# HGRN2's chunk scan on TensorE: four groups of matmuls for each of the first seven heads, in place of sixteen small steps

## The chip, the cores and the metric

The kernel runs on one core of a Trainium2 chip. The metric is device time in microseconds of one execution, the median of the runs shown. A core has TensorE (PE, matmuls, with weight loads shown as PEld), VectorE (DVE), ScalarE (ACT), GpSimd (POOL) and SyncE (SP), which issues most of the DMAs. Each engine works through its own list of instructions in the order in which the program gives them, and waits on semaphores for the others.

## The reference

One step of a two-layer decoder: 512 prompt tokens and 64 sample tokens (8 sequences of 8), width 1024. Layer 0 mixes tokens by HGRN2, layer 1 by S5; each layer has a SwiGLU and an embedding part behind it. The change touches only HGRN2, which has 8 heads of 128 and computes, chunk by chunk:

```python
def step(s, xs):
    qc, kc, vc, lc = xs
    b = jnp.cumsum(lc, axis=1)
    bm = b[:, CHUNK // 2 - 1][:, None]
    bl = b[:, -1]
    qh = qc * jnp.exp(b - bm)
    kh = kc * jnp.exp(bm - b)
    att = jnp.where(causal, jnp.einsum('bthk,bshk->bhts', qh, kh), 0.0)
    o = (jnp.einsum('bhts,bshv->bthv', att, vc)
         + jnp.einsum('bthk,bhkv->bthv', qc * jnp.exp(b), s))
    s_new = (jnp.exp(bl)[..., None] * s
             + jnp.einsum('bshk,bshv->bhkv', kc * jnp.exp(bl[:, None] - b), vc))
    return s_new, o
...
q, fz, v, g = jnp.split(x @ w_in, 4, axis=-1)
f = lbf + (1.0 - lbf) * jax.nn.sigmoid(fz)
qh = heads(jax.nn.silu(q) * HG_QK_SCALE)
kh = heads(1.0 - f)
o, s = hgrn2_chunk_scan(qh, kh, heads(v), heads(jnp.log(f)), s0)
o = rms_norm(o, gnorm_w) * jax.nn.silu(heads(g))
return o @ w_out, s
```

The prompt starts from a zero state, the eight samples from stored ones; the new states are outputs (`hgp`, `hgs`).

## The kernel before, in words

The whole program is written in the order in which it is issued (`manual_schedule`); the functions below are Python generators, and where each yields decides what stands next to what on every engine.

All large products are done in three matmuls each (`mm3`, lines 299 to 301): a weight is split into a high and a low part (`whi`, by ScalarE on line 200, and `wlo`, by VectorE on line 203), and so is the input. Weights arrive by DMA from SP (`wraw`, line 226), 512 KB at a time, two buffers deep, and are split some steps ahead; `passed` counts the matmul triples and issues these splits.

`proj(h)` makes the projections of head h: for even h first V for two heads (40 triples of 256 columns), then in every head decay, query and gate, each 8 triples of 320 columns and 8 of 256. So an even head has 88 steps (n = 0 to 87) and an odd one 48. Behind each of the three a side generator is queued, `decay`, `factors` or `queries`, which does the elementwise work on ScalarE, VectorE and GpSimd, one piece per step. `decay` makes the exponentials `e`, `L` and `k` and four running sums `b`. `factors` makes KH, QH, KL, QL, K2 and E2. `queries` starts with nine empty steps (`QWAIT`), so it runs early in the next head's projections; it copies the gates, applies SiLU (with a table load ahead and one behind), and gives QH, QL and Q2 their final values.

The scan of head h is interleaved with the projections of head h + 1: the loop at the end of `hgrn` advances `scan(h)` after the steps listed in `SCAN_AT` (line 66), the first row beside even projections, the second beside odd ones. So scans of even heads run beside odd projections, which have fewer steps. A scan has these steps, with the lines by which the profile names them:

- transposes of K2, four tiles (L661) and the samples' tile (L668), each copied to `kT` by ScalarE
- kT x V (L674), and the chunk states `S` on VectorE; `hgp` is written
- the samples' state updates (L688), one into a `tr` bank and one into an `mm` bank, and `So` on VectorE in two halves; `hgs` is written
- scores in four steps: KH x QH for a tile of 128 tokens (L704) and seven small products KL x QL of 16, 32 and 64 columns (L709); then VectorE copies the unmasked part to `att` (L713)
- samples: Q2 x S0 (L719), copied to `oc`; their score (L725), copied to `ats` (L727)
- output: L732, L735 and, two steps later, L741 and L743; ScalarE squares it
- the mean square (L752), then `r` by Ln and Exp on ScalarE, and the scaling on VectorE

The kernel uses eight banks of PSUM: four `mm` for projections, two `tr`, one `o` and one `os` for the scan. A tile is a whole bank and the banks of a tag go round in turn. The program waits by tile: a matmul into a bank waits for the engine that last read that tile, whatever columns it read.

The last head's scan runs beside the output projection (`mix_out`, line 809).

Of the kernel before, what the change touches and what calls it, by code (L numbers as in the profile page):

```python
# [8 lines left out]
FP32 = mybir.dt.float32  # L9
# [3 lines left out]
ACT = mybir.ActivationFunctionType  # L13
OP = mybir.AluOpType
# [3 lines left out]
T = 576  # L18
NB = 288
NP = 512  # L20

HC = ((0, 320), (320, 576))
H = 8
# [39 lines left out]
SY = ((6, 8), (8, 8), (6, 10), (6, 2))  # L63
QY = ((3, 3), (2, 5), (1, 3), (1, 2))
SPLIT_S5 = 14
SCAN_AT = ((2, 4, 10, 16, 20, 26, 30, 34, 38, 42, 46, 50, 54, 60, 68, 74), (2, 4, 6, 9, 12, 15, 17, 19, 21, 23, 26, 33, 34, 36, 41, 45))
QWAIT = 9
SIDE = 1
OCT = 2
# [73 lines left out]
def hybrid_decoder_kernel(ctx: ExitStack, tc: tile.TileContext, a: dict):  # L143
    nc = tc.nc
# [6 lines left out]
    def bank(tag, bufs):  # L151
        return psum.tile([128, 512], FP32, tag=tag, name=tag, bufs=bufs)

    def mm_bank():
        return bank("mm", 4)

    def tr_bank():
        return bank("tr", 2)
# [3 lines left out]
    ident = cst[:, 0:128]  # L162
    vmask = cst[:, 128:132]
    idpat = cst[:, 136:152]
    gnw = cst[:, 152:153]
# [6 lines left out]
    EPS_LN, EPS_RMS, ONE, ZERO = (eps[:, i:i + 1] for i in range(4))  # L172
    ones = {}
# [13 lines left out]
    xfh = xf_t.rearrange("p (k c) -> p k c", k=KD)  # L187
# [8 lines left out]
    def act(out, in_, func, bias=None, scale=1.0):  # L196
        nc.scalar.activation(out, in_, func, bias=ZERO if bias is None else bias, scale=scale)  # L197

    def copy(out, in_):
        nc.scalar.activation(out, in_, ACT.Copy)  # L200

    def tt(out, x, y, op, eng=None):
        (eng or nc.vector).tensor_tensor(out, x, y, op=op)  # L203

    def stt(out, x, s, y, op0, op1):
        nc.vector.scalar_tensor_tensor(out, x, s, y, op0=op0, op1=op1)
# [148 lines left out]
    def run(g):  # L355
        for _ in g:
            pass

    def step(g, n=1):
        for _ in range(n):  # L360
            if next(g, StopIteration) is StopIteration:
                return False
        return True
# [109 lines left out]
    def hgrn():  # L473
        es = ExitStack()
        hp = es.enter_context(tc.tile_pool(name="hp", bufs=1))
        msk = hp.tile([128, 224], FP32, name="msk")
        nc.sync.dma_start(msk, a["cst"][:, 160:384])
        own = msk[:, 192:224]
        attm = msk[:, None, 0:128].bitcast(U32).to_broadcast([128, 4, 128])
        smask = msk[:, 128:192].bitcast(U32)  # L480
# [8 lines left out]
        att_sb, ats_sb = [], []  # L489
# [18 lines left out]
        def t576(tag, bufs=1):  # L508
            return hp.tile([128, T], FP32, tag=tag, name=tag, bufs=bufs)

        V = {}
        hd = {}
        sides = []
# [12 lines left out]
        def proj(h):  # L526
            if h % 2 == 0:
                p = take(16)
                V[h // 2] = hp.tile([128, 5, 256], FP32, tag="V", name="V", bufs=2)
                for i in range(5):  # L530
                    c = slice(i * 128, i * 128 + 128) if i < 4 else slice(T - 128, T)
                    ps = mm_bank()
                    for k in range(KD):
                        hi, lo = w_ap(p + 2 * k, 256)
                        mm3(ps[:, :256], xhih[:, k, c], xloh[:, k, c], hi, lo, k == 0, k == KD - 1)
                        yield
                    copy(V[h // 2][:, i, :], ps[:, :256])
                free_to(p + 16)
            d = hd[h] = {}

            yield from two_units(take(8))
            sides.append(decay(h, d, hd["ps"]))

            yield from two_units(take(8))
            sides.append(factors(d, hd["ps"]))
            yield from two_units(take(8))
            sides.append(queries(h, d, hd["ps"]))
# [12 lines left out]
        LEVELS = list(enumerate((16, 32, 64)))  # L560
# [92 lines left out]
        def scan(h):  # L653
# [106 lines left out]
            tt(o[:, NP:], ops[:, 0:64], r[:, NP:], OP.mult)  # L760
            yield

        nc.scalar.preload_act_table_set(LNEXP)
        g = None
        for h in range(H):
            at = SCAN_AT[h % 2]
            for n, _ in enumerate(proj(h)):
                if n % SIDE == 0 and sides and not step(sides[0]):
                    sides.pop(0)
                for _ in range(at.count(n) if g else 0):  # L770
                    step(g)
            if g:
                run(g)
            g = scan(h)

        xq.close()
        XS.append(ctx.enter_context(tc.tile_pool(name="xs", bufs=1, side="right")))
# [30 lines left out]

    def mix_out():
        es, g = hgrn()  # L810
        p0 = take(64)
        held = []
# [941 lines left out]
    with more_weights(3, (pos["i"] + 64) // 8):  # L1754
        start = ple_gate(1, pj, pp, SEGS, y_emit, GW[1])
# [140 lines left out]
```

## Time and profile before

| | |
|---|---|
| median of three runs | 1588.85 us (1588.47 to 1592.74) |
| profiled execution | 1589.6 us, its span 1587.8 us |
| TensorE busy | 1514.9 us, 95% |
| VectorE, ScalarE, GpSimd busy | 60%, 43%, 22% |
| mean granted clock of TensorE | 0.983 |
| scans of the first seven heads | from 50 to 312 us of the span |

A row of the timeline gives start, length, engine, line, operation, output<-inputs, shape and count; in square brackets stands the idle time of the engine ahead of it and what ended it. TensorE's fp32 matmuls are shown as two records each (L704, L741 and the like), the transposes as one. Matmuls overlap in the pipeline, so the distance from one start to the next tells their price, not their length. A row of the waits gives who waited for whom, the sum in us, how often, and the longest.

### The profile page before, as it was taken

Reading aid. Unit: us, or ns where it says so; the run is one execution under the profiler, and the core shown is the slowest. Engines: PE = TensorE matmul, PEld = TensorE weight load, DVE = VectorE, ACT = ScalarE, POOL = GpSimd, SP = SyncE. Lnnn points to the kernel's source line nnn. Section 1 sums busy time; section 2 is a strip of 40 time slices with the busy share of each in tenths; the row PEclk is TensorE's granted clock in tenths of the full one; section 3 lists DMA queues with packets and bytes.
Section 4 is the critical chain, followed back from the end, with each engine's and each line's share of the span. In section 5 each row is a group of like instructions: output and inputs, shape, how many; then the busy total and the mean of one; then the engine's idle time right before and its main releaser. Section 6 shows DMA issues by size and latency. Waiting matters only on the chain. (4 is left out here: it accounts for less than half of the span.)

```text
span 1587.8 us, 30040 instructions
## 1 busy us (share of the span) xinstructions
PE 1514.9 (95%) x12550; PEld 1467.1 (92%) x12550; DVE 947.1 (60%) x1711; ACT 687.9 (43%) x1152; POOL 342.9 (22%) x447
## 2 busy tenths in 40 slices
PE   8899999899999999999999947999999999999998
PEld 7898989788999999999989947899999999999997
DVE  4848484868547778953486699457433233334685
ACT  5546464746532223123278524436432222123375
POOL 1303030302003768860022332302000000000111
PEclk9999999999999999999999978999999999999999
DMA  5223131232224877663214986432222222223121
GB/s 185 95 69 101 63 109 64 100 115 80 68 70 145 216 185 216 195 182 108 98 54 170 233 209 179 101 107 80 67 80 93 80 81 93 81 80 120 31 78 60
DMA packets 97255, 180.32 MB, mean 114 GB/s; under 512 B 41888, under 2 KB 56912, under 8 KB 96864
## 3 DMA queue, kind: packets, MB, share of 16 engines
q1 hardware_dynamic: 88144, 151.92, 31.3%
q0 software_dynamic: 8976, 26.49, 6.2%
q8 instruction: 98, 1.61, 0.4%
q14 instruction: 37, 0.30, 0.1%
HBM read 151.08 MB, written 27.30 MB: 112 GB/s over the span
## 5 line engine op out<-in xcount | busy, mean ns | idle before, releaser
L299 PE MATMUL mm<-xh,whi 128*128 128x288 f32 x2048 | 609.7, 298 | 9.5 <-ACT xh L200 6.5
L300 PE MATMUL mm<-xl,whi 128*128 128x288 f32 x2048 | 608.9, 297 | 5.0 <-POOL xl L203 3.5
L301 PE MATMUL mm<-xh,wlo 128*128 128x288 f32 x2048 | 606.6, 296 | 1.3 <-DVE wlo L203 1.3
L299 PEld LDWEIGHTS mm<-xh,whi 128*128 128x128 f32 x2048 | 387.8, 189 | 15.9 <-ACT xh L200 7.6
L300 PEld LDWEIGHTS mm<-xl,whi 128*128 128x128 f32 x2048 | 387.9, 189 | 8.4 <-POOL xl L203 5.0
L301 PEld LDWEIGHTS mm<-xh,wlo 128*128 128x128 f32 x2048 | 387.8, 189 | 1.5 <-DVE wlo L203 1.5
L200 ACT ACTIVATE whi<-wraw 128x1024 fp32r<-128x1024 f32 x208 | 218.7, 1053 | 250.1 <-DMA wraw<-in_w_dram 117.2
L203 DVE TENSOR_TENSOR wlo<-wraw,whi 128x1024 fp32r<-128x1024 f32 x200 | 247.1, 1252 | 33.2 <-ACT whi L200 32.8
L299 PE MATMUL mm<-hhi,whi 128*128 128x288 f32 x704 | 209.3, 297 | 0.0
L301 PE MATMUL mm<-hhi,wlo 128*128 128x288 f32 x704 | 207.5, 295 | 0.0
L300 PE MATMUL mm<-hlo,whi 128*128 128x288 f32 x704 | 207.2, 294 | 0.0
L203 DVE TENSOR_TENSOR fs<-fs,mm 128x288 f32<-128x288 f32 x88 | 39.9, 454 | 254.5 <-PE mm L301 241.4
L203 POOL TENSOR_TENSOR ln_s<-ln_s,xf 128x288 f32<-128x288 f32 x24 | 24.3, 1012 | 570.9 <-DVE xf L203 451.2
L299 PEld LDWEIGHTS mm<-hhi,whi 128*128 128x128 f32 x704 | 132.1, 188 | 1.7 <-issue 1.4
L300 PEld LDWEIGHTS mm<-hlo,whi 128*128 128x128 f32 x704 | 132.1, 188 | 0.3
L301 PEld LDWEIGHTS mm<-hhi,wlo 128*128 128x128 f32 x704 | 132.0, 188 | 0.0
L299 PE MATMUL mm<-xhi,whi 128*128 128x320 f32 (+1 forms) x384 | 121.5, 316 | 0.0
L300 PE MATMUL mm<-xlo,whi 128*128 128x320 f32 (+1 forms) x384 | 113.3, 295 | 0.0
L301 PE MATMUL mm<-xhi,wlo 128*128 128x320 f32 (+1 forms) x384 | 113.2, 295 | 0.0
L200 ACT ACTIVATE hhi<-fs 128x288 fp32r<-128x288 f32 x88 | 38.8, 441 | 152.1 <-DVE fs L203 152.1
L197 ACT ACTIVATE fs<-mm,eps 128x288 f32<-128x288 f32 x88 | 44.1, 502 | 131.0 <-PE mm L301 130.9
L299 PEld LDWEIGHTS mm<-xhi,whi 128*128 128x128 f32 x384 | 72.7, 189 | 6.9 <-issue 4.4
(318 smaller groups left out, 2273.9 us busy)
## 6 DMA issues: line engine op xcount, KB each, us to landing
wraw<-in_w_dram SPq DMA_DIRECT2D x198, 512.0 KB
wraw<-in_w_dram POOLq DMA_DIRECT2D x10, 512.0 KB, 7.1
S<-in_s_dram SPq DMA_DIRECT2D x8, 512.0 KB
out_hgs_dram<-So SPq DMA_DIRECT2D x8, 512.0 KB
wr<-wt_scratch SPq DMA_DIRECT2D x16, 256.0 KB
bT<-in_s5bt_dram SPq DMA_DIRECT2D x16, 256.0 KB
cl_scratch<-cl POOLq DMA_DIRECT2D x16, 256.0 KB, 6.1
zw_scratch<-zw POOLq DMA_DIRECT2D x16, 256.0 KB, 6.5
```

The source lines that it names most:

```text
L197: nc.scalar.activation(out, in_, func, bias=ZERO if bias is None else bias, scale=scale)
L200: nc.scalar.activation(out, in_, ACT.Copy)
L203: (eng or nc.vector).tensor_tensor(out, x, y, op=op)
L299: nc.tensor.matmul(out, whi, rhi, start=start, stop=False)
L300: nc.tensor.matmul(out, whi, rlo, start=False, stop=False)
L301: nc.tensor.matmul(out, wlo, rhi, start=False, stop=stop)
```

## The change

Seven of the eight heads get a new generator, `grouped_scan`; head 7 keeps `scan`. The matmuls are the same in number and shape. Their order is new, in four groups between which projections run:

1. all five transposes, all scores (KH x QH for four tiles, then the small products tile by tile), the samples' Q2 x S0 and their score
2. kT x V and both state updates
3. the whole output
4. the mean square

The generator has seven steps; `GROUP_AT` says after which projection steps it advances: beside even projections at 24, 32, 36, 40, 48, 56 and 62, beside odd ones at 18, 24, 27, 30, 34, 39 and 44. Before, a scan began at step 2 and ended at 74 or 45. The scores move from a `tr` bank to the `o` bank. The samples' transpose, their Q2 x S0 and their score, three `tr` banks before, share one bank (`ps1`) at columns 0, 256 and 128. The state half in the `mm` bank is taken up first.

```diff
-SCAN_AT = ((2, 4, 10, 16, 20, 26, 30, 34, 38, 42, 46, 50, 54, 60, 68, 74), (2, 4, 6, 9, 12, 15, 17, 19, 21, 23, 26, 33, 34, 36, 41, 45))
+GROUP_AT = ((24, 32, 36, 40, 48, 56, 62), (18, 24, 27, 30, 34, 39, 44))
...
+        def grouped_scan(h):
...
+            while "Q2" not in d:
+                run(sides.pop(0))
...
+            ps, ps1, sc = tr_bank(), tr_bank(), bank("o", 1)
+            for j in range(4):
+                nc.tensor.transpose(ps[:, j * 128:j * 128 + 128], K2[:, j * 128:j * 128 + 128], ident)
+            copy(kT[:, 0:4, :], ps.rearrange("p (j k) -> p j k", j=4))
+            nc.tensor.transpose(ps1[:, 0:128], K2[:, T - 128:T], ident)
+            copy(kT[64:128, 4, :], ps1[64:128, 0:128])
+            for j in range(4):
+                o = j * 128
+                nc.tensor.matmul(sc[:, o:o + 128], KH[:, o:o + 128], QH[:, o:o + 128], start=True, stop=True)
+            for j in range(4):
+                for i, l in LEVELS:
+                    for n in range(64 // l):
+                        q0 = i * 256 + j * 64 + n * l
+                        s0 = 2 * l * n
+                        nc.tensor.matmul(sc[s0:s0 + l, j * 128 + s0 + l:j * 128 + s0 + 2 * l],
+                                         KL[:, q0:q0 + l], QL[:, q0:q0 + l], start=True, stop=True)
+            att, ats = att_sb[h % 2], ats_sb[h % 2]
+            nc.vector.copy_predicated(att, attm, sc.rearrange("p (j k) -> p j k", j=4))
+            for q in range(8):
+                c, o = NP + 32 * (q // 4), 256 + 128 * (q // 4)
+                nc.tensor.matmul(ps1[32 * (q % 4):32 * (q % 4) + 32, o:o + 128],
+                                 Q2[:, c:c + 32], S0[:, q, :], start=True, stop=True)
+            nc.tensor.matmul(ps1[64:128, 128:192], KH[:, NP:T], QH[:, NP:T], start=True, stop=True)
+            oc = hp.tile([128, 2, 128], FP32, tag="oc", name="oc")
+            copy(oc, ps1[:, 256:512].rearrange("p (r v) -> p r v", r=2))
+            nc.vector.copy_predicated(ats[64:128, :], smask[64:128, :], ps1[64:128, 128:192])
+            yield
+            ps = tr_bank()
+            for j in range(4):
+                nc.tensor.matmul(ps[:, j * 128:j * 128 + 128], kT[:, j, :], Vh[:, j, :], start=True, stop=True)
+            pss = [tr_bank(), mm_bank()]
+            for half, p in enumerate(pss):
+                r = slice(64 + 32 * half, 96 + 32 * half)
+                nc.tensor.matmul(p, kT[r, 4, :], vm[r].rearrange("p q v -> p (q v)"), start=True, stop=True)
+            S = hp.tile([128, 4, 128], FP32, tag="S", name="S")
+            copy(S[:, 0, :], ps[:, 0:128])
+            for j in range(1, 4):
+                stt(S[:, j, :], S[:, j - 1, :], E2[:, j * 128 + 127:j * 128 + 128], ps[:, j * 128:j * 128 + 128],
+                    OP.mult, OP.add)
+            nc.sync.dma_start(a["hgp"][h], S[:, 3, :])
+            yield
+            So = hp.tile([128, 8, 128], FP32, tag="So", name="So")
+            for half in (1, 0):
+                for i in range(4):
+                    q = 4 * half + i
+                    stt(So[:, q, :], S0[:, q, :], E2[:, NP + 8 * q + 7:NP + 8 * q + 8],
+                        pss[half][:, i * 128:i * 128 + 128], OP.mult, OP.add)
+                yield
+            nc.sync.dma_start(a["hgs"][h], So)
+            ops, ob = bank("os", 1), bank("o", 1)
+            for r in range(2):
+                nc.tensor.matmul(ops[:, 32 * r:32 * r + 32], oc[:, r, :], own, start=r == 0, stop=False,
+                                 skip_group_check=True)
+            nc.tensor.matmul(ops[:, 0:64], Vh[64:128, 4, :], ats[64:128, :], start=False, stop=True,
+                             skip_group_check=True)
+            for j in range(4):
+                o = j * 128
+                nc.tensor.matmul(ob[:, o:o + 128], Vh[:, j, :], att[:, j, :], start=True, stop=j == 0)
+                if j:
+                    nc.tensor.matmul(ob[:, o:o + 128], S[:, j - 1, :], Q2[:, o:o + 128], start=False, stop=True)
+            sq = t576("sq")
+            act(sq[:, NP:], ops[:, 0:64], ACT.Square)
+            act(sq[:, :NP], ob, ACT.Square)
+            yield
+            r = t576("r")
+            pss = [tr_bank(), tr_bank()]
+            for blk in range(2):
+                c = slice(blk * NB, blk * NB + NB)
+                nc.tensor.matmul(pss[blk][:, :NB], ones[128], sq[:, c], start=True, stop=True)
+                act(r[:, c], pss[blk][:, :NB], ACT.Ln, bias=EPS_RMS)
+            act(r, r, ACT.Exp, scale=-0.5)
+            yield
+            stt(r, r, gnw, d["gs"], OP.mult, OP.mult)
+            o = xfh[:, h, :]
+            tt(o[:, :NP], ob, r[:, :NP], OP.mult)
+            tt(o[:, NP:], ops[:, 0:64], r[:, NP:], OP.mult)
+            yield
...
         for h in range(H):
-            at = SCAN_AT[h % 2]
+            at = GROUP_AT[h % 2]
...
-            g = scan(h)
+            g = (scan if h == H - 1 else grouped_scan)(h)
```

On TensorE, here is the end of head 2's scores beside projection 3. Before, a score block (L704, L709), two projection steps and the samples' Q2 x S0 (L719), with the semaphores that an instruction waits for:

```order
L704 MATMUL tr<-QH,KH 128x128
L709 MATMUL tr<-QL,KL 16x16 x4
L709 MATMUL tr<-QL,KL 32x32 x2
L709 MATMUL tr<-QL,KL 64x64
L299 MATMUL mm<-xhi,whi 128x320
L300 MATMUL mm<-xlo,whi 128x320
L301 MATMUL mm<-xhi,wlo 128x320
L299 MATMUL mm<-xhi,whi 128x320
L300 MATMUL mm<-xlo,whi 128x320
L301 MATMUL mm<-xhi,wlo 128x320
L719 MATMUL tr<-S_1289,Q_1447 32x128 [waits DMAHW7_49,DVE_49,PE_49]
L719 MATMUL tr<-S_1289,Q_1447 32x128 x7
```

Now the same place: the last tile's small products (L790), Q2 x S0 (L796) and the samples' score (L798), all within the first group.

```order
L790 MATMUL o<-QL,KL 16x16 x4
L790 MATMUL o<-QL,KL 32x32 x2
L790 MATMUL o<-QL,KL 64x64
L796 MATMUL tr<-S_1288,Q_1411 32x128 [waits DMAHW7_49,DVE_49,Activation_49]
L796 MATMUL tr<-S_1288,Q_1411 32x128 x7
L798 MATMUL tr<-QH,KH 64x64
L299 MATMUL mm<-xhi,whi 128x320
```

The projection steps between have gone elsewhere, and Q2 x S0 waits for ScalarE (`Activation`), whose value there is that of the copy of kT's fifth tile out of the same bank.

On ScalarE, beside projection 3 before, from the copies of kT to a weight's conversion (`whi`); `qg` are the gates, the row between the table loads is SiLU:

```order
L200 ACTIVATE kT<-tr 128x512 [waits PE_49]
L200 ACTIVATE kT<-tr 64x128 [waits PE_49]
L200 ACTIVATE S<-tr 128x128 [waits DMAHW2_49,PE_49]
L200 ACTIVATE qg<-mm 128x320
L200 ACTIVATE qg<-mm 128x256
L197 ACT_TABLE_LOAD
L197 ACTIVATE qg<-qg,eps 128x1152 [waits Activation_49]
L641 ACT_TABLE_LOAD
L200 ACTIVATE whi<-wraw 128x1024 [waits DMAHW0_49,PE_49]
```

Now, from SiLU on; `e`, `L` and `k` are the decay of head 3, the projection being computed:

```order
L197 ACTIVATE qg<-qg,eps 128x1152 [waits Activation_49]
L641 ACT_TABLE_LOAD
L200 ACTIVATE whi<-wraw 128x1024 [waits DMAHW0_49,PE_49]
L197 ACTIVATE e<-mm,eps 128x320
L197 ACTIVATE e<-mm,eps 128x256 [waits PE_49]
L197 ACTIVATE L<-e,eps,lbt 128x576 [waits DVE_49]
L197 ACTIVATE e<-e,eps 128x576 [waits Activation_49]
L197 ACTIVATE k<-L,eps 128x576 [waits DVE_49,Pool_49]
L200 ACTIVATE kT<-tr 128x512 [waits PE_49]
L200 ACTIVATE kT<-tr 64x128 [waits PE_49]
L200 ACTIVATE oc<-tr 128x256 [waits PE_49]
```

The copies of kT stood ahead of the gates' SiLU; they now stand behind it, behind a conversion and behind the next head's decay up to `k`.

On ScalarE beside even projections, around step 56, before: the decay of head 4, then the squares and `r` of head 3's scan.

```order
L197 ACTIVATE L<-e,eps,lbt 128x576 [waits DVE_49]
L197 ACTIVATE e<-e,eps 128x576 [waits Activation_49]
L197 ACTIVATE k<-L,eps 128x576 [waits DVE_49,Pool_49]
L197 ACTIVATE sq<-os,eps 128x64
L197 ACTIVATE sq<-o,eps 128x512 [waits PE_49]
L197 ACTIVATE r<-tr,eps 128x288 [waits PE_49] x2
L197 ACTIVATE r<-r,eps 128x576 [waits Activation_49]
```

Now:

```order
L197 ACTIVATE e<-mm,eps 128x256 [waits PE_49]
L197 ACTIVATE r<-tr,eps 128x288 [waits DVE_49,PE_49]
L197 ACTIVATE r<-tr,eps 128x288 [waits PE_49]
L197 ACTIVATE r<-r,eps 128x576 [waits Activation_49]
L197 ACTIVATE L<-e,eps,lbt 128x576 [waits DVE_49]
L197 ACTIVATE e<-e,eps 128x576 [waits Activation_49]
L197 ACTIVATE k<-L,eps 128x576 [waits DVE_49,Pool_49]
```

The squares stand further ahead, and `r` has come in front of `L`.

More of the change, by code (lines that the diff above doesn't have):

```diff
@@ L761, in scan @@
             yield
+        def grouped_scan(h):
+            d = hd.pop(h)
+            Vh = V[h // 2][:, :, (h % 2) * 128:(h % 2) * 128 + 128]
+            while "Q2" not in d:
+                run(sides.pop(0))
+            KH, QH, KL, QL, K2, E2, S0, Q2 = (d[n] for n in ("KH", "QH", "KL", "QL", "K2", "E2", "S0", "Q2"))
+            kT = hp.tile([128, 5, 128], FP32, tag="kT", name="kT")
+            vm = hp.tile([128, 4, 128], FP32, tag="vm", name="vm")
+            nc.gpsimd.tensor_tensor(vm[64:128], Vh[64:128, 4:5, :].to_broadcast([64, 4, 128]),
+                                    vmask[64:128, :, None].to_broadcast([64, 4, 128]), op=OP.mult)
+            ps, ps1, sc = tr_bank(), tr_bank(), bank("o", 1)
[75 more added lines that the diff above has]
+            yield
```

## The prediction

> **What bounds the kernel now.** I read the page first, then TensorE's waits, then the timelines of TensorE, ScalarE and VectorE around one head's scan, and last the granted clock window by window. The profiled execution took 1589.6 us, 0.75 above the median of the runs shown (1588.85), and its span is 1587.8.
>
> ```profile
> PE 1514.9 (95%) x12550; PEld 1467.1 (92%) x12550; DVE 947.1 (60%) x1711; ACT 687.9 (43%) x1152; POOL 342.9 (22%) x447
> ...
> PE tr L661 <- DVE K L203: 9.3, 4, 3.9
> ```
>
> TensorE is busy for 95% of the span, so time is won only where TensorE idles or does something shorter. Its longest wait inside the scans is for K2 at the first transposes (L661): 9.3 us in four, the longest 3.9. All four are scans of even heads, which run beside an odd head's projections. Odd heads' scans wait nowhere. These rows are TensorE beside projection 3 (scan of head 2), and the same place beside projection 1:
>
> ```profile
> 126.90 0.31 PE L301 MATMUL mm<-xhi,wlo 128*128 128x320 f32 x1
> 129.00 0.66 PE L661 MATMUL tr<-cst,K 128*128 128x128 f32 x4 [1.79 <-DVE K L203]
> ...
> 131.38 1.05 PE L674 MATMUL tr<-V,kT 128*128 128x128 f32 x8
> ...
> 136.44 0.28 PE L299 MATMUL mm<-xhi,whi 128*128 128x256 f32 x1
> ...
> 136.79 0.47 PE L704 MATMUL tr<-QH,KH 128*128 128x128 f32 x2
> 137.19 0.92 PE L709 MATMUL tr<-QL,KL 128*16 128x16 f32 x14
> ...
> 138.59 0.31 PE L299 MATMUL mm<-xhi,whi 128*128 128x320 f32 x1
> ...
> 139.03 0.38 PE L704 MATMUL tr<-QH,KH 128*128 128x128 f32 x2
> 139.34 0.56 PE L709 MATMUL tr<-QL,KL 128*16 128x16 f32 x14
> 139.83 0.42 PE L299 MATMUL mm<-xhi,whi 128*128 128x320 f32 x1
> 140.08 0.31 PE L300 MATMUL mm<-xlo,whi 128*128 128x320 f32 x1
> ...
> 151.65 0.60 PE L741 MATMUL o<-att,V 128*128 128x128 f32 x4
> 152.09 0.39 PE L743 MATMUL o<-Q,S 128*128 128x128 f32 x2
> ...
> 50.44 1.02 PE L661 MATMUL tr<-cst,K 128*128 128x128 f32 x4 [3.89 <-DVE K L203]
> ...
> 54.37 0.83 PE L674 MATMUL tr<-V,kT 128*128 128x128 f32 x6
> ```
>
> Starts give the prices. A projection step (three matmuls) is 0.44 us with 320 columns (138.59 to 139.03) and 0.35 with 256 (136.44 to 136.79). A 128-column pass of the scan is 0.11 (four from 151.65 to 152.09). One score block is 0.31 for KH x QH, of which 0.2 is the change from 128 to 16 columns, then 0.49 for the fourteen small passes (139.34 to 139.83), and 0.10 more on the way out (139.83 to 140.08 against a plain 0.15). The first block's small passes take 0.85: they wait 0.36 for QL.
>
> **Joining the groups.** The four score blocks cost 4 x 0.90 = 3.6 us. Now eight KH x QH passes (0.88), one change of width (0.1 beyond a pass) and 4 x 0.49 make 2.95: 0.65 less. (The step from 64 columns back to 16 stands in no row; I take it at what the 0.49 holds for the step to 128.) Where the same group goes on to the samples and to the last score matmul, and where the three pieces of the output become one, about five edges of 0.1, like the one on the way out, go: 0.5 by estimate. Transposes, kT x V, the states and the RMS sums only stand elsewhere; their passes remain, and a full-width group shows hardly any edge. That is 1.15 per head, 8.1 for seven, between 0.6 x 7 = 4.2 (only the scores gain) and 11.
>
> **The waits that go.** By starts, TensorE stood still for 129.00 - 126.90 - 0.15 = 1.95 us in each of three scans and about 3.9 in the first: 9.8. The wait for QL, 4 x 0.36 = 1.4, goes too. The first stall is followed by half clock: from L661 to L674 it is 3.93 us (50.44 to 54.37) against 2.38 (129.00 to 131.38), so 1.5. Removed in all: 8.1 + 9.8 + 1.4 + 1.5 = 20.8 us.
>
> **When TensorE reaches the new first group.** Beside an odd projection it stands after step 18. From 127.05, where step 2 ends, sixteen steps follow: 8 x 0.44 + 8 x 0.35 = 6.3, so 133.4; five transposes bring it to 133.95. Then it needs QH, and for the samples (L796) it needs Q2 and a ScalarE semaphore. The last is the copy of kT's fifth tile: it reads the bank into which L796 writes. By the Trainium skill (PSUM — Partial Sum Buffer, "PSUM bank collisions raise a hardware error") two engines may not use one bank on the same 32 partitions at once, whatever the columns, so the wait belongs to this layout; no run here shows it otherwise. These are ScalarE and VectorE before:
>
> ```profile
> 111.55 0.88 ACT L197 ACTIVATE e<-mm,eps 128x320 f32<-128x320 f32 x2
> 112.95 0.87 ACT L197 ACTIVATE L<-e,eps,lbt 128x576 f32<-128x576 f32 x1 [0.53 <-DVE e L568]
> ...
> 118.04 0.99 ACT L197 ACTIVATE r<-tr,eps 128x288 f32<-128x288 f32 x2 [0.97 <-PE tr L752]
> 119.06 0.78 ACT L197 ACTIVATE r<-r,eps 128x576 f32<-128x576 f32 x1
> 119.74 1.05 ACT L200 ACTIVATE whi<-wraw 128x1024 fp32r<-128x1024 f32 x1
> ...
> 127.08 0.78 ACT L197 ACTIVATE K<-K,eps 128x576 f32<-128x576 f32 x1 [1.99 <-DVE K L203]
> ...
> 130.57 0.87 ACT L200 ACTIVATE kT<-tr 128x512 f32<-128x512 f32 x2
> ...
> 132.64 0.71 ACT L200 ACTIVATE qg<-mm 128x320 f32<-128x320 f32 x2
> ...
> 134.66 1.26 ACT L197 ACTIVATE qg<-qg,eps 128x1152 f32<-128x1152 f32 x1
> ...
> 138.20 0.88 ACT L197 ACTIVATE e<-mm,eps 128x320 f32<-128x320 f32 x2
> ...
> 142.39 0.78 ACT L197 ACTIVATE k<-L,eps 128x576 f32<-128x576 f32 x1 [0.89 <-DVE L L203]
> ...
> 48.30 0.76 ACT L197 ACTIVATE K<-K,eps 128x576 f32<-128x576 f32 x1
> ...
> 114.66 0.76 DVE L203 TENSOR_TENSOR L<-L,e 128x576 f32<-128x576 f32 x1 [1.74 <-ACT e L197]
> ...
> 125.36 1.68 DVE L203 TENSOR_TENSOR K<-b 128x512 f32<-128x512 f32 x2
> ...
> 135.96 0.76 DVE L206 SCALAR_TENSOR_TENSOR QH<-qg,QH 128x576 f32<-128x576 f32 x1 [0.17 <-ACT qg L197]
> ...
> 139.34 0.46 DVE L568 TENSOR_SCALAR e<-e 128x576 f32<-128x576 f32 x1
> ```
>
> First stall, for QH. The chain is VectorE's, without a gap from L (114.66) to K (125.36), then the exponential of K2 at 127.08. In an even projection the scan's r now stands on ScalarE ahead of L, and r takes 119.74 - 118.04 = 1.7. L can start at 112.43 + 1.7 = 114.1 instead of 112.95: everything behind is 1.2 later, so K2's exponential is at 128.3. From there to the copies of kT ScalarE needed 130.57 - 127.08 = 3.5; kT and S are no longer there, the gate copies follow at once, and from them to the end of SiLU is 135.92 - 132.64 = 3.3. SiLU ends at 135.1, QH 0.8 later at 135.9. TensorE has waited since 133.95: 1.95 us. For head 0 no r stands ahead: SiLU ends at 48.30 + 6.8 = 55.1, QH at 55.9. TensorE got to L661 at 50.44 - 3.89 = 46.55, so it is through the transposes at 46.55 + 6.85 = 53.4 and waits 2.5. Four scans: 3 x 1.95 + 2.5 = 8.4.
>
> Second stall, for kT. The copies of kT now stand on ScalarE behind SiLU, a weight's conversion and the next head's decay up to the exponential k, and that one needs VectorE twice. From the end of SiLU: the decay's first exponentials end 139.08 - 135.92 = 3.2 later; from VectorE's e to k is 142.39 - 139.34 = 3.05; k and the two copies are 0.7 + 0.87. The fifth tile is copied 7.8 after SiLU, at 142.9. TensorE is at L796 0.98 + 4 x 0.49 = 2.95 after QH, at 138.85. It stands for 4.0 us, the same in all four scans, because both ends hang on SiLU: 16.0. The bounds: nothing, if ScalarE should come to the copies by 138.85; and 5.2, if the weight's conversion ahead of them waits once more (1.06) for its load.
>
> Even projections. There the copies of kT stand behind copies of V that wait for TensorE itself, and the group is later (step 24): no stall. Group two follows six or eight steps (2.1 us or more) behind and finds kT done; the output needs S, the sums need the squares, with 3.8 and 2.2 us of steps between. SP issues hgp and hgs later, behind the weights' loads of that stretch; POOL's mask product has no deadline before group two. All at nothing, under TensorE's projection steps; each would cost at most what it is late.
>
> **The clock.** Work of TensorE and granted clock, window by window (us of the window, busy, clock, DMA):
>
> ```profile
> 47.17:50.58 3.41, 0.14 (x1) 1.00 0.65 240
> 50.58:54.00 3.42, 3.42 (x15) 0.50 0.27 68
> 125.67:129.08 3.41, 1.61 (x12) 1.00 0.15 61
> 129.08:132.50 3.42, 3.42 (x27) 1.00 0.13 28
> ...
> 313.41:316.82 3.41, 1.40 (x9) 1.00 0.05 18
> 316.82:320.23 3.41, 3.41 (x11) 0.50 0.08 24
> 320.23:323.65 3.42, 3.42 (x16) 0.50 0.00 0
> ```
>
> A window of 3.41 us with 1.61 us of work leaves the clock full, one with 1.40 halves the next. A stall of 4.0 us leaves at least 2.0 idle in one window, thus at most 1.4 of work. The next window then runs at half; what lies in it behind the stall is lost by half: 0.65 to 1.7 us, on average over where the window begins 1.4. Four times: 5.6.
>
> **The sum.** 8.4 + 16.0 + 5.6 - 20.8 = 9.2 us more; 1589.6 + 9.2 = 1598.8 as profiled, 1598.0 beside the median. That is 0.6%; about 0.3% (4.8 us) is what a measurement of this kernel can tell from no change.
>
> **Rivals.**
>
> ScalarE comes in time (faster). Were the copies of kT done by 138.85, the second stall and its half clocks go: 9.2 - 16.0 - 5.6 = -12.4, 1576. For it: odd heads' scans, where ScalarE has room, show no wait. Against it: the order puts k ahead of the copies, and k needs VectorE's L. It decides at 4 us: ScalarE would have to be that much ahead of the chain above. Stalls of half the size, without lost clock, still give 9.2 - 8 - 5.6 = -4.4. Chance 0.2.
>
> The stalls come, the clock stays full. Then 9.2 - 5.6 = 3.6: 1592, not to be told from no change. For it: 1.61 of work was enough, 0.2 above what the stall leaves at its worst split. Against it: the row with 1.40. By the Trainium skill (TensorE: Matmul & The Clock Gate, "What's actually happening") half rate follows after at least one idle window of about 3.4 us; a stall of 4.0 would rarely hold a whole one, and the time would be this rival's. The row with 1.40 speaks against that reading. Chance 0.15.
>
> More half clock, or nothing won by joining (slower still). At 316.82 two windows ran at half. A second one after each stall is 4 x 1.7 = 6.8: 1605. The same, nearly, if joined groups save nothing and the 8.1 stay. For it: the two stalls of a scan lie 3 us apart and may share a window. Against: work is dense behind. Chance 0.15.
>
> **How the numbers follow.** The forecast has 0.5, and its own range, from the bounds of joining (4.2 to 11) and a us of the chain to each side (four times), is 1593 to 1604. The range 1585 to 1605 holds that, the full clock, most of the case above, and the stalls of half the size; most of the case of ScalarE in time is left out. Faster by over 0.3% has 0.2 from that case; within 0.3% 0.17, the full clock and the lower edge of the forecast; slower 0.63.
>
> **What would show it.** L778 waits for nothing; L784 waits about 2 us for QH in four scans and L796 about 4 us for ScalarE's kT in the same four, with half clock behind; no wait of that size in the three scans beside even projections, nor at the second to fourth groups. If L796 has no wait, the forecast is wrong by its main term; if it has and the clock stays full, by 5.6.

## The result, and the profile after

The changed kernel took 1610.7 us (median of four runs, 1608.21 to 1613.36) against 1588.66 (1587.69 to 1592.74) for the kernel before, measured beside it: 1.0129 times as long, interval 1.0108 to 1.015. The profiled execution took 1612.2 us, its span is 1610.4; before it was 1587.8. The forecast was slower, by 9; it is slower by 22. The page of the profile after, first lines:

```profile
span 1610.4 us, 30078 instructions
...
PE 1515.6 (94%) x12550; PEld 1472.1 (91%) x12550; DVE 949.1 (59%) x1711; ACT 688.0 (43%) x1152; POOL 344.1 (21%) x447
...
PEclk9998989899999999999999978999999999999999
```

The number of matmuls is the same and so, nearly, is TensorE's busy time. The row of the clock has three eights in its first eight slices that were nines before. TensorE's waits from 40 to 330 us of the span, which hold the seven scans:

```profile
PE tr L796 <- ACT kT L200: 13.3, 4, 3.8
PE o L784 <- DVE QH L206: 6.3, 4, 1.6
PE mm L299 <- ACT qg L200: 4.9, 3, 1.6
```

The wait for K2 (9.3 us) is gone. In its place stand the two that were forecast, at L784 and L796 in four scans each, and one that was not: a projection's matmul (L299) that waits for a bank until ScalarE has copied the gates out of it. This is TensorE beside projection 3, the place that the prediction worked out:

```profile
133.59 0.41 PE L299 MATMUL mm<-xhi,whi 128*128 128x320 f32 x1 [1.64 <-ACT qg L200]
...
137.31 1.13 PE L784 MATMUL o<-QH,KH 128*128 128x128 f32 x8 [1.58 <-DVE QH L206]
138.37 2.72 PE L790 MATMUL o<-QL,KL 128*16 128x16 f32 x56
144.22 1.08 PE L796 MATMUL tr<-S,Q 128*32 128x128 f32 x16 [3.13 <-ACT kT L200]
```

Three times in 11 us TensorE stands. ScalarE over the same stretch, from the preceding projection's decay to the copies of kT:

```profile
112.83 0.88 ACT L197 ACTIVATE e<-mm,eps 128x320 f32<-128x320 f32 x2
113.60 0.89 ACT L197 ACTIVATE r<-tr,eps 128x288 f32<-128x288 f32 x2
...
129.63 0.78 ACT L197 ACTIVATE K<-K,eps 128x576 f32<-128x576 f32 x1 [0.72 <-DVE K L203]
...
135.12 1.26 ACT L197 ACTIVATE qg<-qg,eps 128x1152 f32<-128x1152 f32 x1
...
142.62 0.78 ACT L197 ACTIVATE k<-L,eps 128x576 f32<-128x576 f32 x1 [0.89 <-DVE L L203]
143.30 0.88 ACT L200 ACTIVATE kT<-tr 128x512 f32<-128x512 f32 x2
```

`r` stands ahead of the decay's `L`, as the new order says, and the copies of kT end at 144.18, 7.8 us behind SiLU (136.38); L796 starts 0.04 later. Windows of the clock over the two stalls (us of the window; TensorE, weight loads, VectorE, ScalarE, GpSimd busy; granted clock, DMA share, GB/s). In all traces of this case the granted clock changes on a grid of 3.41 us, so a stretch at half clock lasts 3.41 us or a multiple of it (6.83, 10.24); the windows below follow that grid to 0.1 us:

```profile
135.40:138.80 3.40, 1.81 (x26) 1.45 (x23) 2.39 (x5) 3.37 (x4) 0.00 (x0) 1.00 0.62 208
138.80:142.20 3.40, 2.30 (x44) 1.61 (x42) 0.94 (x3) 2.37 (x4) 0.00 (x0) 0.51 0.02 5
142.20:145.60 3.40, 1.38 (x18) 0.88 (x18) 2.67 (x4) 1.53 (x3) 0.00 (x0) 0.50 0.00 0
145.60:149.00 3.40, 3.40 (x14) 3.36 (x13) 2.81 (x4) 0.38 (x1) 0.00 (x0) 0.50 0.00 0
```

Three windows in a row run at half clock (0.51, 0.50, 0.50), the last of them full of work. The prediction had reckoned with one.

### The profile page after: what moved, and what is told of

Same layout as the page of the kernel before. It is cut to its first block, busy times and chain, and to the rows that moved or that the text cites. A ratio compares the mean times of both kernels' runs of the same rounds, so it can differ in the third digit from the quotient of the medians.

```text
span 1610.4 us, 30078 instructions
## 1 busy us (share of the span) xinstructions
PE 1515.6 (94%) x12550; PEld 1472.1 (91%) x12550; DVE 949.1 (59%) x1711; ACT 688.0 (43%) x1152; POOL 344.1 (21%) x447
## 3 DMA queue, kind: packets, MB, share of 16 engines
q8 instruction: 98, 1.61, 0.4%
## 4 chain that ended last, share of the span: by engine, by line
PE 75%; DVE 12%; ACT 7%; DMA 2%; issue 2%; POOL 1%; SPq 0%; DVEq 0%; ACTq 0%; POOLq 0%
PE mm L299 23%; PE mm L300 23%; PE mm L301 23%; ACT whi L200 1%; DVE wlo L203 1%; DVE pr L203 1%; DVE b L580 1%; DVE xl L203 1%; DVE xf L203 1%; DMA wraw<-in_w_dram 1%; ACT e L197 1%; DVE ln_z L203 1%; DVE ln_q L203 1%; PE mm L1568 1%; PE o L835 0%
## 5 line engine op out<-in xcount | busy, mean ns | idle before, releaser
L299 PE MATMUL mm<-xh,whi 128*128 128x288 f32 x2048 | 610.7, 298 | 11.6 <-ACT xh L200 8.3
L299 PEld LDWEIGHTS mm<-xh,whi 128*128 128x128 f32 x2048 | 388.9, 190 | 17.4 <-ACT xh L200 9.7
L299 PE MATMUL mm<-hhi,whi 128*128 128x288 f32 x704 | 209.3, 297 | 0.0
L299 PEld LDWEIGHTS mm<-hhi,whi 128*128 128x128 f32 x704 | 132.1, 188 | 1.7 <-issue 1.4
L299 PE MATMUL mm<-xhi,whi 128*128 128x320 f32 (+1 forms) x384 | 119.2, 310 | 4.9 <-ACT qg L200 4.9
L299 PEld LDWEIGHTS mm<-xhi,whi 128*128 128x128 f32 x384 | 74.7, 195 | 9.6 <-ACT qg L200 5.7
```

What stands on the lines that cost most here:

```text
L299: nc.tensor.matmul(out, whi, rhi, start=start, stop=False)
```

## The experiments

Twelve runs, each timed against the kernel before on the same chip; the kernel before had medians of 1588.3, 1588.7, 1589.3 and 1589.7 us in the four groups of runs. My theory: the loss is the wait at L796, made by a bank that the fifth transpose shares with the samples, and the half clock behind it. Rivals: the place of group one, or the output's and the sums' earlier place beside even projections. Lines behind the fifth transpose are one higher wherever it has the os bank.

**The fifth transpose in the os bank.**

```diff
-            nc.tensor.transpose(ps1[:, 0:128], K2[:, T - 128:T], ident)
-            copy(kT[64:128, 4, :], ps1[64:128, 0:128])
+            pk = bank("os", 1)
+            nc.tensor.transpose(pk[:, 0:128], K2[:, T - 128:T], ident)
+            copy(kT[64:128, 4, :], pk[64:128, 0:128])
```

> The changed kernel, but the fifth transpose goes to the os bank instead of sharing a bank with the samples' products; nothing else. Theory A (beside odd projections TensorE stands before Q2 x S0 only because ScalarE's copy of kT reads the same bank, and that copy stands behind the next head's decay): the wait of 3.1 to 3.8 us at Q2 x S0 is gone in all four scans, kT x V waits at most 0.5 us, and with less half clock the time falls by 14 us for the stalls and 4 to 9 for the clock, to 1588 to 1593. Rival B (the loss comes from the joined small matmuls themselves, which the clock gate takes for too little work, or from the late decay): the wait goes, but half clock and time stay, 1605 or more.

1593.6 us, ratio 1.0027 (1.0013 to 1.004), 0.6 above the range expected. Its waits and two clock windows around group one:

```profile
PE o L785 <- DVE QH L206: 5.9, 4, 1.6
PE tr L848 <- ACT sq L197: 5.2, 4, 1.3
PE mm L299 <- ACT qg L200: 4.9, 3, 1.6
```

```profile
126.60:130.00 3.40, 2.14 (x14) 1.90 (x14) 2.48 (x2) 3.37 (x5) 1.44 (x1) 1.00 0.46 154
130.00:133.40 3.40, 2.15 (x47) 1.85 (x48) 2.43 (x5) 3.37 (x5) 0.00 (x0) 1.00 0.47 159
```

The wait at L796 (L797 here) is gone, and with it every half clock of the seven scans: 17 us of the 22. The copies of kT are as late as ever (7.8 us behind SiLU); only nobody waits for them. The two first stalls remain and cost no clock. A new wait, of 1.3 us for the squares, has appeared. So the wait at L796 belongs to the layout. The Trainium skill (PSUM — Partial Sum Buffer, "PSUM bank collisions raise a hardware error") has two engines kept apart by bank and quadrant. What the trace shows is the program's own wait for the tile: with another bank the 3.1 to 3.8 us are gone; no run here lets two engines into one bank.

**Group one beside odd projections three steps earlier.**

```diff
-GROUP_AT = (..., (18, 24, 27, 30, 34, 39, 44))
+GROUP_AT = (..., (15, 24, 27, 30, 34, 39, 44))
```

> The changed kernel with the first group beside odd projections after step 15 instead of 18, ahead of the next head's decay, so that ScalarE copies kT right behind SiLU's second table load. Theory A: no wait at Q2 x S0 (the copy is done 2.2 us after SiLU, TensorE comes 3.75 after it), while the wait for QH grows by three steps of 0.44 us; 2.7 us less in each of four scans, 11 in all, and 4 to 9 for the clock: 1591 to 1597. Rival B: 1605 or more. If the place were too early in itself (waits for QH decide), the time would rise above 1610.7.

Missed: 1614.7 us, 1.0156 (1.0134 to 1.0178). The copies of kT do come ahead of the next head's decay, but TensorE now waits for QH all at once:

```profile
PE o L784 <- DVE QH L206: 18.0, 4, 4.8
```

```profile
130.90:134.30 3.40, 0.52 (x5) 0.28 (x3) 3.17 (x2) 3.37 (x6) 2.05 (x2) 0.99 0.32 102
```

A stall of 4.8 leaves a window with 0.52 us of work, and 10.24 us at half clock follow each of the four. I had let the wait for QH grow by 1.3 us; it grew by 3.2, since QH does not come earlier and the 1.6 us that TensorE stood for the gates' bank now fall into it. The squares are waited for as well (6.5 us in three scans), so the waits sum to 24.5 us, as in the change (13.3, 6.3 and 4.9).

**The groups beside even projections only**, the old steps beside odd ones.

```diff
-            at = GROUP_AT[h % 2]
+            at = SCAN_AT[1] if h % 2 else GROUP_AT[0]
...
-            g = (scan if h == H - 1 else grouped_scan)(h)
+            g = (grouped_scan if h % 2 and h < H - 1 else scan)(h)
```

> The new groups only for the scans beside even projections (heads 1, 3 and 5); heads 0, 2, 4, 6 and 7 scan as before in sixteen steps. Joining alone gives 3 x 1.1 = 3.3 us, so 1585.4, if nothing else of the change acts on the odd projections. Theory C (moving output and r ahead of the decay makes the next odd projection's TensorE come 1.5 us earlier and its K2 and queries 1.2 us later): the waits for K2 grow by 2.7 us in three scans, 8 in all, and the time is 1593 to 1595, slower than before.

1599.1 us, 1.0063 (1.0044 to 1.0081), more than either reading gave, and nearer to the one in which the even groups make the odd stretches late. Beside odd projections nothing was changed, yet the old wait for K2 has grown:

```profile
PE tr L662 <- DVE K L204: 17.1, 4, 4.6
```

```profile
129.74 1.12 PE L662 MATMUL tr<-cst,K 128*128 128x128 f32 x4 [4.58 <-DVE K L204]
```

It was 1.79 beside projection 3; it is 2.79 more. Half clock follows it in all four. `r` ahead of `L` on ScalarE explains 1.27 of it (below); the other 1.5 were missing in my sum.

**The even output, sums and scaling late.**

```diff
-GROUP_AT = ((24, 32, 36, 40, 48, 56, 62), ...
+GROUP_AT = ((24, 32, 36, 40, 60, 68, 74), ...
```

> The changed kernel with the last three steps beside even projections after steps 60, 68 and 74, where they stood before the change, instead of 48, 56 and 62. Theory C: r stands behind the decay again and the output group after step 55, so the waits for the gates' bank and for QH shrink from 3.6 us to about 0.9 in three scans: 8 us less, about 1602; the wait for kT stays at 3 to 4. If that move costs nothing, 1610 as the changed kernel.

1596.4 us, 1.005 (1.0028 to 1.0073): 14 less than the change, where I had expected 8.

```profile
PE tr L796 <- ACT kT L200: 15.2, 4, 3.8
PE o L784 <- DVE QH L206: 1.6, 1, 1.6
```

The waits for the gates' bank, and for QH in three of four scans, are gone. L796 waits its full 3.8 each time, since L790 no longer runs at half clock, and only 6.83 us at half clock follow each instead of 10.24.

**Only the even sums and scaling late**, the output at 48 as in the change.

```diff
-GROUP_AT = ((24, 32, 36, 40, 48, 56, 62), ...
+GROUP_AT = ((24, 32, 36, 40, 48, 68, 74), ...
```

> The changed kernel, but beside even projections only the sums with r and the scaling go back to steps 68 and 74; the output group stays at 48. It parts the two halves of what the output-late run undid. If r ahead of L makes the chain 1.2 us late and the output group ahead of the decay lets TensorE come 1.56 us early, the waits for the gates' bank and QH fall from 3.3 to about 2.1 in three scans and the time by 3 to 5 us, to 1605 to 1608. If r is all of it, the time is 1596 to 1600; if the output group is, 1610.

1604.4 us, 1.01 (1.0082 to 1.0117), 0.6 under the range expected if both halves matter, and outside of what either alone would give (1596 to 1600, or 1610).

```profile
PE o L784 <- DVE QH L206: 6.3, 4, 1.6
PE mm L299 <- ACT qg L200: 1.1, 3, 0.4
```

With `r` out of the way the gates' wait falls from 1.6 to 0.4 in each, by 1.2; the other 2.0 (0.4 and 1.6) needed the output moved.

**The os bank and the even output late together.**

> The fifth transpose in the os bank and the last three steps beside even projections after 60, 68 and 74; beside odd ones as in the changed kernel (18 on). If what e1 and e4 took away adds up, the waits for the gates' bank and QH, 3.3 us together, are left in the first scan alone, and the time is 8 us under that with the os bank alone: 1581 to 1585. The waits for the squares (1.3 us in four scans) stay or grow to 2, since TensorE comes earlier.

> The version with the os bank and the even output late, once more beside the one with the odd output at 32, on the same chip: 1578 to 1582 by its first measurement, the wait at L848 3 to 4 us in all.

1580.4 us, 0.9943 (0.9924 to 0.9961), and again 1582.0, 0.9946 (0.9926 to 0.9967): faster than before, by about the 8 us that the joined groups were to give. TensorE's waits from 40 to 320 us of the span sum to 9.1 and 11.7 us in the two runs, against 11.4 before, so what is won is in the main the joining. The largest wait left is the one for the squares (3.9 and 5.2 us, where the second run was expected to show 3 to 4). ScalarE, in the first of the two runs, beside projection 3:

```profile
146.20 0.78 ACT L197 ACTIVATE KH<-d,eps 128x576 f32<-128x576 f32 x1 [3.47 <-DVE d L203]
146.88 0.76 ACT L197 ACTIVATE QH<-d,eps 128x576 f32<-128x576 f32 x1
147.55 0.29 ACT L197 ACTIVATE sq<-os,eps 128x64 f32<-128x64 f32 x1
147.75 0.68 ACT L197 ACTIVATE sq<-o,eps 128x512 f32<-128x512 f32 x1
```

The squares stand behind the next head's KH and QH, and those wait for VectorE's `d`, itself behind the states S and So of this scan.

**The same with the odd groups later.** Three ways of giving the copies more time beside odd projections, all with the os bank and the even output late:

```diff
-(18, 24, 27, 30, 34, 39, 44)
+(18, 26, 28, 31, 35, 42, 46)
```

> As the run with the os bank and the output late, but beside odd projections the groups behind the first at 26, 28, 31, 35, 42 and 46 instead of 24, 27, 30, 34, 39 and 44. The sums come 1.1 to 1.3 us later, so the wait for the squares falls from 1.3 to 2 us to under 0.8: 3 to 5 us less than with 24 to 44, 1577 to 1581. If the squares' wait only moves along, no difference.

```diff
-(18, 24, 27, 30, 34, 39, 44)
+(18, 24, 27, 30, 41, 45, 47)
```

> The fifth transpose in the os bank, even rows with the last three steps at 60, 68, 74, odd rows with the output, sums and scaling at 41, 45, 47 in place of 34, 39, 44; the first four odd steps stay at 18, 24, 27, 30. In the run with the output at 34 TensorE waited 3.9 us in all at L848 for the squares, which stood on ScalarE behind the next head's KH and QH exponentials. Theory A: the output at 41 is issued when ScalarE has those behind it, as in the run with odd rows from 26 on, where L848 waited for nothing; then 1575 to 1579 and no wait at L848. Theory B: the next head's exponentials fill ScalarE wherever the output stands; then the wait stays or goes to r and the scaling, and the time is 1580 to 1583.

```diff
-(18, 24, 27, 30, 34, 39, 44)
+(26, 33, 36, 38, 41, 45, 47)
```

> The fifth transpose in the os bank, the last three steps beside even projections after 60, 68 and 74, and beside odd projections all steps later: 26, 33, 36, 38, 41, 45 and 47. Theory A and C together: no wait of over 0.5 us for K2, QH, the gates' bank or kT in any of the seven scans, no half clock there, so the kernel before less 8 us for joining and 12 for its own waits and half clock: 1568 to 1573, up to 1580 if the squares come late for the sums. Rival B (joined groups cost by themselves): no better than the run with the os bank alone, about 1590.

The first took 1579.3 us (0.9946, 0.9926 to 0.9965), in the expected range, but not the 3 to 5 less that it was for: no difference to the run without it can be told. The second took 1587.8 (0.9994, 0.9984 to 1.0004) and the third 1590.0 (1.001, 1.0001 to 1.002), both misses (for the second, outside of what either theory gave). Their largest waits, one row from each in this order:

```profile
PE tr L848 <- ACT sq L197: 6.3, 4, 1.6
```

```profile
PE tr L848 <- ACT sq L197: 9.8, 4, 2.5
```

```profile
PE tr L811 <- DVE ats L802: 9.1, 4, 3.3
```

An output that is issued later finds more of the next head's exponentials ahead of its squares: with 41 all six of them. The third's 1590 is the number of the rival, by which joined groups cost by themselves; the runs with the same joined groups at 1579.3 and 1580.4 rule that cause out. In the third run group one itself is late, and its copies `att` and `ats` fall behind the next head's running sums and a weight's split on VectorE:

```profile
138.73 3.85 DVE L580 TENSOR_TENSOR_SCAN b<-seg,L 128x576 f32<-128x576 bf16 x3
...
144.35 0.23 DVE L802 COPY_PREDICATED ats<-msk,tr 64x64 f32<-64x64 uint32 x1
```

L811 takes the bank that `ats` is read from, so it waits till 144.6. In the runs with group one at 18 `att` and `ats` stand ahead of the three running sums.

**Is that wait the cause?** The third with group two five steps later:

```diff
-(26, 33, 36, 38, 41, 45, 47)
+(26, 38, 40, 41, 43, 46, 47)
```

> The os bank, even rows as above, odd rows 26, 38, 40, 41, 43, 46, 47: group one late as in the run that missed (1590.0), but group two at 38 in place of 33. Theory A: that run lost 9.1 us because the states' first product (L811) takes the bank that VectorE's copy ats still reads, and that copy stands behind the next head's three running sums (3.85 us) and a weight's split; it ended 3 us after TensorE wanted the bank. Five steps (2 us) more give most of it back and with it the half clock behind: 1576 to 1583, L811 under 1 us in each. Theory B: the late place itself costs it (head 7's scan, the stretch behind it) and the wait at L811 only shows it: 1588 to 1592, with the wait gone or not.

1589.9 us, 1.0006 (0.9994 to 1.0017). The wait at L811 falls from 9.1 to 1.1, and nothing is won. That is the rival's number; its cause, the late place in itself, is not shown by it:

```profile
PE o L838 <- ACT S L200: 7.5, 4, 2.0
...
PE tr L811 <- DVE ats L802: 1.1, 1, 1.1
```

The first copy of S now stands behind the exponentials on ScalarE, and the output waits for that. My theory of this miss falls in the form in which I gave it: the wait was true, but it was one of several in a row.

**The squares ahead of the next head.** The version with the os bank and the even output late, and one number changed:

```diff
-(18, 24, 27, 30, 34, 39, 44)
+(18, 24, 27, 30, 32, 39, 44)
```

> The fastest version so far (os bank, even output, sums and scaling at 60, 68, 74; 1580.4) with one number changed: the output beside odd projections at 32 in place of 34. In ScalarE's order the two squares then stand ahead of the next head's KH and QH exponentials; with 34 they stood behind those, which wait for VectorE, and with 41 behind six of them (TensorE waited 3.9 and 9.8 us in all at L848). Theory A, that each group's copy is late by what stands ahead of it in its engine's order: no wait at L848, 3 to 5 us less than with 34, 1575 to 1578. Theory B, that the wait only moves again (to S at L838, since VectorE makes the states at 142.3 to 143.3 and the output would come at 142.4): 1579 to 1584.

1577.0 us, 0.9916 (0.9896 to 0.9936): 5.0 less than the same kernel without it in the same group of runs, and the shortest of all. ScalarE beside projection 3:

```profile
142.01 0.69 ACT L197 ACTIVATE sq<-o,eps 128x512 f32<-128x512 f32 x1 [1.18 <-PE o L838]
144.09 0.78 ACT L197 ACTIVATE KH<-d,eps 128x576 f32<-128x576 f32 x1 [1.39 <-DVE d L203]
```

The squares stand ahead of KH and are ready 1.39 us before it; TensorE waits for them nowhere, 5.2 us less in four scans than in the same group's run without it. Two steps earlier did what one and seven steps later could not.

## Why the prediction was wrong in size

The sign and the stalls came as forecast, the size not: 1598.0, with a range to 1605, against 1610.7. The step that failed is the term for the clock: one window at half clock behind each stall, 5.6 us in all, where two or three followed, 12.9 us. The stalls up to L784 were also too small (8.4 against 11.2), and the stretch behind head 6's scan stood at nothing (6.9). Up to head 7's scan the terms compare thus (us):

| term | forecast | measured |
|---|---|---|
| joined groups | -8.1 | -8.4 |
| waits for K2 and QL | -11.2 | -11.2 |
| stalls up to L784 | +8.4 | 6.3 + 4.9 = +11.2 |
| stall at L796 | +16.0 | +13.3 |
| half clock, less the 1.5 of before | +4.1 | +10.8 |
| sum to head 7's scan | +9.2 | +15.7 |
| head 7's scan and the output projection | 0 | +3.4 |
| behind | 0 | +3.5 |

The last rows come from the same instruction in both traces, head 7's first transposes and a sum behind the output projection; first before:

```profile
312.13 0.38 PE L661 MATMUL tr<-cst,K 128*128 128x128 f32 x2
...
324.06 0.49 PE L704 MATMUL tr<-QH,KH 128*128 128x128 f32 x2 [0.22 <-DVE QH L206]
...
397.18 0.69 PE L434 MATMUL tr<-ln_q,ones 128*128 128x288 f32 x1
```

and after:

```profile
327.86 0.49 PE L661 MATMUL tr<-cst,K 128*128 128x128 f32 x3
...
339.12 0.49 PE L704 MATMUL tr<-QH,KH 128*128 128x128 f32 x2 [2.64 <-DVE QH L206]
...
416.27 1.17 PE L434 MATMUL tr<-ln_q,ones 128*128 128x288 f32 x2
```

That is 15.7 and 19.1; the spans differ by 22.6. The joined groups' 8.4 is measured beside even projections and taken for all seven; the 11.2 is what the waits for K2 and QL took before, and neither is left; the half clock's 10.8 is what the 15.7 leave.

**Joining: right.** Beside an even projection, where nothing waits, group one shows its prices:

```profile
91.79 1.06 PE L784 MATMUL o<-QH,KH 128*128 128x128 f32 x8
92.78 2.04 PE L790 MATMUL o<-QL,KL 128*16 128x16 f32 x56
94.75 0.64 PE L796 MATMUL tr<-S,Q 128*32 128x128 f32 x16
```

Eight KH x QH take 0.99 (forecast 0.98), the small products 1.97 (4 x 0.49). From its first matmul to that of the next projection, projection 2 with head 1's scan takes 43.03 us (82.41 to 125.44), and 44.23 before (81.49 to 125.72), both without a wait: 1.2 per head against 1.15.

**The stall at L796: its chain right to the tenth, its size 13.3 for 16.0.** From the exponential of K2 to the end of SiLU I forecast 6.8, it is 136.38 - 129.63 = 6.75; from there to the copies 7.8, it is 7.80. The idle time is 3.8 in the first scan and 3.1 to 3.2 in the others, where L790 runs partly at half clock (2.72 for 2.04) and fills the difference. The run with the os bank takes this wait away and needs no other cause for it.

**The stall for QH: mis-sized, an edge overlooked.** `r` delays K2 as forecast: from `e` to K2's exponential 16.80 after against 15.53 before, 1.27 for 1.2. But I took TensorE's time of arrival from before, where the last part of the output is done behind the start of the even projection's decay (`e` at 111.55); before, beside projection 2:

```profile
112.70 0.61 PE L741 MATMUL o<-att,V 128*128 128x128 f32 x4
...
114.04 0.39 PE L743 MATMUL o<-Q,S 128*128 128x128 f32 x2
```

The change puts the whole output ahead of it (in the trace after it ends at 109.2, and `e` starts at 112.83), so TensorE has some 1.5 us less to do while the decay's chain runs, and comes that much too early. 1.64 + 1.58 = 3.22 in three scans is the measure, not 1.95; the wait for QH in the first is 1.58, not 2.5 (TensorE came there at 54.1, not 53.4, and SiLU ended at 54.75, not 55.1). The run with the even groups only shows the same on the old scan (2.79 = 1.27 + 1.5), and the pair with the sums late and with the output late too takes the two parts away one after the other. A part of it met the gates' bank (L299) first, a wait that I had not looked for.

**The half clock: the step that failed most.** "The next window then runs at half; what lies in it behind the stall is lost by half ... on average 1.4." In three scans it is three windows with 2.30 + 1.38 + 3.40 = 7.08 us of work, in the first 1.19 + 3.40 (60 to 67 us): 12.9 us lost (half clock lasts 10.24 us in each of the three, and the other two hold 7.06 and 7.03 us of work), 11.4 without the 1.5 of before; the sum above leaves 10.8. Two things were wrong. The stalls before L784 take work out of the window ahead (1.81 left), so the half clock begins before the second stall; and the window with the second stall, thin itself, is followed by another half one. I had seen that the two stalls might share a window and kept it for a rival (1605), at a chance of 0.15. In the run with the even output late, where the first stalls are gone in three scans, 6.83 at half clock follow and not 10.24. How the windows fall matters too: with the os bank the same two stalls left 2.14 and 2.15 us of work and lost no clock. The three scans are one case rather than three, since L784 starts 81.8 us apart in them (137.31, 219.07, 300.88), close to 24 windows.

By the Trainium skill (TensorE: Matmul & The Clock Gate, "What's actually happening") half rate follows after at least one idle window of about 3.4 us. The runs decide against that reading here: no stall was that long beside the window with 1.81 us of work, and half rate followed it; the rival that was built on the rule gave 1592.

**What I left at nothing.** Head 7's scan waits for QH, 2.64 instead of 0.22, but that alone costs nothing: from L661 to there TensorE takes 11.26 us, against 11.93 before, when this stretch ran at half clock (316.82 to 323.65) and TensorE came later for that reason. The 3.4 arise behind it. From L704 to L434 it is 77.15 us against 73.12, with half clock for 11.2 us (from 340.2 on, right behind that wait, from 374.4 and from 411.9) against 5.3. What brings these windows about, and the rest, I have not told apart. The 3.5 us behind the output projection are lost in layer 1, where no instruction was changed: behind L434 TensorE stands idle for 50.2 us instead of 47.2, while half clock lasts 37 us in both. Why it does so was not tried, and stays open.

The rivals: ScalarE did not come in time; the clock did not stay full; "more half clock" was right in kind, short by 6.

## What to carry to other kernels

When work is gathered into groups for one engine, follow each copy and each elementwise step of a group to its place in the order of the engine that runs it: it is as late as what stands ahead of it there, and moving it later can put more ahead of it (squares behind six exponentials), while two steps earlier put nothing there. Work that is moved from behind the start of a chain to ahead of it brings its consumer forward by its whole length; take arrival times from the new order, not from the old trace. Where a program waits by bank, as this one does, products that share a bank share its waits, so a copy that nobody needs yet may still stop the next matmul.

## What the runs showed of the hardware

How much of a window TensorE may stand without losing clock is not one number in these traces. Windows of 3.4 us with 1.61 us of work (before) and 2.14 and 2.15 (os bank) were followed by full clock; the one with 1.81 above was followed by half, and so was this one in the run with the os bank and the even output late (head 0):

```profile
53.00:56.40 3.40, 1.90 (x36) 1.60 (x35) 2.43 (x5) 3.37 (x5) 0.30 (x1) 1.00 0.73 201
56.40:59.80 3.40, 3.40 (x51) 2.39 (x50) 1.22 (x2) 2.02 (x4) 0.00 (x0) 0.50 0.00 0
```

The stall in it is 1.5 us. The profile of the second measurement of that same kernel has a window with less work at the same place, and keeps full clock behind it:

```profile
53.86:57.27 3.41, 1.83 (x26) 1.47 (x24) 2.33 (x5) 3.38 (x4) 0.71 (x1) 1.00 0.80 249
```

The window ahead of the one with 1.81 (132.00 to 135.40 after) holds 1.81 us of work as well, and was followed by full clock. So neither the work in a window, as the profile counts it, nor the number of matmuls decides by itself; what does is open.
